# Depthwise convolution over 31 taps: three convolutions of half length over even tokens, odd tokens and their sum

## The chip, the cores and the metric

The kernel runs on one core of a Trainium2 chip. The metric is the device time of one execution in microseconds, the median of several runs. A core has five engines that work side by side, each through its own queue in order: TensorE (PE in the profile, PEld for its weight loads), VectorE (DVE), ScalarE (ACT), GpSimd (POOL) and SyncE (SP, which here only issues DMAs). TensorE writes into PSUM, from where VectorE or ScalarE must fetch the result before the bank is used again.

## The reference

One layer of a block with two branches that share an input projection; 1024 tokens, 1024 channels, 256 context tokens, all in float32. Cut to what matters here:

```
h  = rms_norm(x, g_pre) * (1 + sc) + sh
ua, gate_a, q, k, v, gate_b, gm = split(h @ w_in)
a, g = split(ua)                          # 1024 channels each
y = a * sigmoid(g)
y = conv(y, conv_w, padding 15) + conv_b  # each channel on its own, 31 taps along the tokens
y = silu(layer_norm(y, ln_g, ln_b)) * silu(gate_a)
y_conv = y @ w_conv_out
y_attn = (attention(q, k, v, ctx) * silu(gate_b)) @ w_attn_out
out = (sigmoid(ga) * y_conv + sigmoid(gb) * y_attn) @ w_out
x   = x + gt * rms_norm(out, g_post)
```

For one channel, output token t is the sum over i of w[i] * y[t + i - 15], where tokens outside 0 to 1023 count as zero.

## The kernel before

The kernel keeps channels on the 128 partitions and tokens along the free dimension, so a channel tile is 128 x 1024 and there are eight of them (KD = 8). Matrix products run on float32 values that are split in a high and a low part, three matmuls for each product (`mm3`, L119); the high part (`whi`) is a cast on ScalarE, the low part (`wlo`) a subtraction, on GpSimd in the first half of the program and on VectorE later (`wl`, L142 and L1397).

The program is written as one stream. `stream` (L172) loads, splits and multiplies one weight tile after the other; each tile is a job of two halves of 512 tokens, each half eight steps of three matmuls into a PSUM tile `ppj` with two buffers. `filler(n)` (L1304) does n such steps. Its jobs are the gates, and for each channel tile j of the convolution a `gate` (tanh on ScalarE to `ts`) and a `value` (`conv_jobs`, L741), which VectorE combines to `y`, the gated input of the convolution.

When `y` of a tile is complete, `conv_taps(j, y)` (L768) puts 31 entries on a list. The first is an activation on ScalarE that multiplies `y` with the middle tap and adds the bias. The other 30 are one `scalar_tensor_tensor` each on VectorE: accumulator = `y` shifted * tap weight + accumulator, over 1009 to 1023 tokens. The accumulator lies in PSUM (`pconv`) for the tiles that are done in the first half, and in SBUF (`acc`) from the moment `in_psum[0]` is set to False (L1384). With the last entry GpSimd adds the tile to `ysum` (for the mean of the layer norm) and it is written to DRAM (`accD`).

`pump(n)` (L737) takes n entries from the list and issues them. Where and how many is written by hand:

- In `work(n)` (L1310), after each step of filler, a share `RATE` of an entry: 0.25 while the context is normalised, 0.45 during `ctx_kv`, 0.2 while the weights of the first group are loaded, 0.5 behind the groups.
- In the loop over 4 groups and 4 quarters (L1348, sixteen blocks): a query/key/value product of 48 matmuls in two halves, then the rope of the block before (`qkv_rope` on VectorE), three entries, then `per` = 20 steps of filler with an entry behind those with i % 5 in (1, 3) and one more where q is odd. At i == 2 the block before is transposed (`qkv_tr`), at i == 4 VectorE and GpSimd make the reciprocal root (`stat`), at i == 9 ScalarE scales (`qkv_scale`, `qk`).
- Behind the loop: entries until none is in PSUM, `work(2)`, the rope of the last block, `work(12)`, its transposes; then one entry per two steps of filler (L1403), five more between the first row maxima, and the rest in `conv_rest` (L1436).

Up to L1394 every engine is held to the order of the program (`Ordered`, L41); behind it the framework may move instructions, with priority for those under `urgent()`. On the convolution follow the layer norm over `accD`, the attention loop, the output projections and the last product.

`gq`, the 64 gains of the query and the key norm, is loaded once at the start (L438, L439). `ctx_kv` uses the key gains (L565), and `rope_tables` (L452) folds both into the tables of the rope. Just behind the first step of `rope_tables` SP issues the weights of group 0 (`wgr`, L584 and L585).

Of the kernel before, what the change touches and what calls it, by code (L numbers as in the profile page):

```python
# [18 lines left out]
P = 128  # L19
D = 1024  # L20
T = 1024
CT = 256
KD = 8
NT = 8
HD = 64
NH = 16
NG = 4
TAPS = 31
PAD = 15
EPS = 1e-6  # L30
SCALE = HD ** -0.5
NKC = (T + CT) // P
# [3 lines left out]
def block_kernel(ctx: ExitStack, tc: tile.TileContext, x, cx, cc, wmod, bmodT, bmodg, vecs, gpost,  # L36
                 wkv, wq, wch, wco, wao, wout, convw, qg, kg, rcos, rsin, out):
    nc = tc.nc
    SP = nc.sync
# [27 lines left out]
    def tl(tag, shape, bufs, dtype=F32, pool="sb"):  # L67
        return pools[pool].tile(list(shape), dtype, tag=tag, bufs=bufs, name=nm(tag))
# [65 lines left out]
    cvb, lng, lnb, gpre = (vec[:, i, :] for i in range(4))  # L134
    bmT = const.tile([P, 16], F32, name="bmT")
    cw = const.tile([P, KD, TAPS], F32, name="cw")
    lngh = const.tile([P, KD], F32, name="lngh")
    lnbh = const.tile([P, KD], F32, name="lnbh")
    gq = const.tile([P, 2, HD], F32, name="gq")


    wl = [G]  # L142
# [295 lines left out]
    SP.dma_start(out=gq[:, 0, :], in_=qg.partition_broadcast(P))  # L438
    SP.dma_start(out=gq[:, 1, :], in_=kg.partition_broadcast(P))  # L439
# [12 lines left out]
    def rope_tables():  # L452
        tcos, tsin = tl("blk", (P, NT, 32), 4, pool="A"), tl("blk", (P, NT, 32), 4, pool="A")
        SP.dma_start(out=tcos[:], in_=rcos)
        SP.dma_start(out=tsin[:], in_=rsin)
        yield 6
        for i in range(2):
            CC = tl("rope", (P, NT, HD), 4, pool="A")
            SS = tl("rope", (P, NT, HD), 4, pool="A")
            for hh in range(2):  # L460
                a, b = hh * 32, (1 - hh) * 32
                V.tensor_tensor(out=CC[:, :, a:a + 32], in0=tcos[:, :, 0:32],
                                in1=gq[:, i, a:a + 32].unsqueeze(1).to_broadcast([P, NT, 32]), op=ALU.mult)
                V.scalar_tensor_tensor(out=SS[:, :, a:a + 32], in0=tsin[:, :, 0:32], scalar=(1.0 if hh else -1.0),
                                       in1=gq[:, i, b:b + 32].unsqueeze(1).to_broadcast([P, NT, 32]),
                                       op0=ALU.mult, op1=ALU.mult)
                yield 2
            rope.append((CC, SS))
# [64 lines left out]
    def ctx_kv():  # L533
# [31 lines left out]
        V.tensor_tensor(out=kv, in0=kv, in1=gq[:, 1, :].unsqueeze(1).to_broadcast([P, 2 * NG, HD]), op=ALU.mult)  # L565
        yield 8
        for gp in range(2):
            p = pt("m", (P, 256))
# [163 lines left out]

    ysum = tl("ysum", (P, T), 1)
    taps = []
    tap_ins = [None]

    def pump(n):  # L737
        for _ in range(min(n, len(taps))):
            taps.pop(0)()

    def conv_jobs(j):  # L741
        st = {}

# [24 lines left out]
    def conv_taps(j, y):  # L768
        st = {}

        def first():
            if not in_psum[0]:
                st["acc"] = tl("acc", (P, T), 2)
            else:
                if j == 0:
                    unshare(1)
                    share({"conv": 1})
                st["acc"] = pt("conv", (P, T))
                in_psum[1] = j + 1
            S.activation(st["acc"][:], y[:], AF.Identity, scale=cw[:, j, PAD:PAD + 1], bias=cvb[:, j:j + 1])  # L780

        def tap(i):
            o = i - PAD
            a, b = max(0, -o), min(T, T - o)
            acc = st["acc"]
            to = acc
            if in_psum[1] == j + 1 and (i == TAPS - 1 or not in_psum[0]):
                st["acc"] = to = tl("acc", (P, T), 2)
                for c, d in ((0, a), (b, T)):
                    if c < d:  # L790
                        S.copy(to[:, c:d], acc[:, c:d])
                in_psum[1] = 0
            tap_ins[0] = V.scalar_tensor_tensor(out=to[:, a:b], in0=y[:, a + o:b + o], scalar=cw[:, j, i:i + 1],
                                                in1=acc[:, a:b], op0=ALU.mult, op1=ALU.add)

        def last():
            acc = st["acc"]
# [7 lines left out]
        for i in range(TAPS):
            if i != PAD:
                taps.append(lambda i=i: tap(i))
        q = taps.pop()
        taps.append(lambda: (q(), last()))

    def tanh_job(src, dst):
        def ev(p, tok):
# [535 lines left out]
    for g in range(NG):  # L1348
        for q in range(4):
            mm = qkv_mm(g, q)  # L1350
            next(mm)
            if prev:
                qkv_rope(*prev)
            else:
                pump(3)
            next(mm)
            next(mm)
            pump(3)
            next(mm)
            due = 0 if q == 3 else 1 if (g, q) == (0, 0) else -1  # L1360
            if q == 2 and g < NG - 1:
# [225 lines left out]
```

## Time and profile before

| | before |
|---|---|
| median of 3 runs | 1412.09 us (1410.0 to 1413.3) |
| the profiled execution | 1411.38 us |
| its span, first to last instruction | 1409.6 us |
| mean granted TensorE clock | 0.989 |
| busy: PE, DVE, ACT, POOL | 1351.9, 1043.1, 564.7, 687.6 us |
| taps with the accumulator in PSUM | 197, 251.9 us of DVE |
| taps into or within SBUF (`acc`) | 43 |
| first and last tap | at 78.9 and 626.4 us |

Times of a row are in microseconds unless they are means of one instruction, which are in nanoseconds. A row of a group names the engine, the operation, the tile written and those read, the shape, the count, then busy time and mean, then the idle time of the engine just ahead of these instructions and what ended it. All engine operations have line L51, that of the helper that records them, so the tiles tell which is which: `pconv` and `acc` are the accumulators of the convolution, `y<-ts,ppj` the gate product, `ts<-ts,ppj` a silu, `ppj` a projection, `po` in the first half the query/key/value product, `ps<-kk,rq` and `mx` the row maxima, `ps<-r,kk` and `pe` the scores. PE counts as busy until the modelled end of a matmul, which overlaps with the next.

### The profile page before, as it was taken

Reading aid. Unit: us, or ns where it says so; the run is one execution under the profiler, and the core shown is the slowest. Engines: PE = TensorE matmul, PEld = TensorE weight load, DVE = VectorE, ACT = ScalarE, POOL = GpSimd, SP = SyncE. Lnnn points to the kernel's source line nnn. Section 1 sums busy time; section 2 is a strip of 40 time slices with the busy share of each in tenths; the row PEclk is TensorE's granted clock in tenths of the full one; section 3 lists DMA queues with packets and bytes.
Section 4 is the critical chain, followed back from the end, with each engine's and each line's share of the span. In section 5 each row is a group of like instructions: output and inputs, shape, how many; then the busy total and the mean of one; then the engine's idle time right before and its main releaser. Section 6 shows DMA issues by size and latency. Waiting matters only on the chain.

```text
span 1409.6 us, 19371 instructions
## 1 busy us (share of the span) xinstructions
PE 1351.9 (96%) x6520; PEld 1000.3 (71%) x6520; DVE 1043.1 (74%) x1359; ACT 564.7 (40%) x1388; POOL 687.6 (49%) x559
## 2 busy tenths in 40 slices
PE   5999999999999999999999999999999999999995
PEld 3768889887888877666666666666666565788774
DVE  3476988998889998885775566567676776349967
ACT  5542344343433332134444445445454434222333
POOL 1112257466556550054675556555556656263623
PEclk9999999999999999999999999999999999999998
DMA  9733434444444436523545444543365657699754
GB/s 317 272 127 105 137 109 159 140 167 150 136 144 134 152 111 185 163 90 116 177 152 171 135 120 147 183 144 120 113 197 173 214 194 263 218 315 347 242 186 154
DMA packets 153187, 242.41 MB, mean 172 GB/s; under 512 B 19792, under 2 KB 72572, under 8 KB 153088
## 3 DMA queue, kind: packets, MB, share of 16 engines
q1 hardware_dynamic: 139648, 218.03, 47.1%
q10 hardware_dynamic: 13440, 23.14, 5.6%
q8 instruction: 52, 0.85, 0.3%
q14 instruction: 47, 0.39, 0.1%
HBM read 161.46 MB, written 79.52 MB: 171 GB/s over the span
## 4 chain that ended last, share of the span: by engine, by line
PE 60%; DVE 16%; issue 7%; POOL 6%; DMA 5%; ACT 4%; SPq 1%; ACTq 1%; POOLq 0%; DVEq 0%
PE ppj L51 26%; PE ps L51 17%; PE po L51 14%; DVE pconv L51 7%; PE pm L51 3%; DVE t L51 2%; POOL wlo L51 2%; DVE qk L51 2%; DMA wm<-in_wmod 1%; DVE qkt L51 1%; POOL opw L51 1%; DVE acc L51 1%; ACT pe L51 1%; DVE r1st L51 1%; POOL y L51 1%
## 5 line engine op out<-in xcount | busy, mean ns | idle before, releaser
L51 PE MATMUL ppj<-t,whi 128*128 128x512 f32 x1728 | 621.0, 403 | 17.2 <-DVE y L51 9.1
L51 PEld LDWEIGHTS ppj<-t,whi 128*128 128x128 f32 x1728 | 327.8, 190 | 124.1 <-issue 36.5
L51 PE MATMUL ppj<-t,wlo 128*128 128x512 f32 x864 | 340.7, 394 | 0.0
L51 DVE TENSOR_REDUCE mx<-ps 128x1 f32<-128x512 f32 (+1 forms) x320 | 199.7, 682 | 109.8 <-PE ps L51 109.2
L51 ACT ACTIVATE pe<-ps 128x512 f32<-128x512 f32 x320 | 188.0, 597 | 191.8 <-PE ps L51 186.8
L51 DVE SCALAR_TENSOR_TENSOR pconv<-y,cw,pconv 128x1016 f32<-128x1016 f32 (+14 forms) x197 | 251.9, 1279 | 6.7 <-ACT pconv L51 2.0
L51 PE MATMUL ps<-r,kk 128*128 128x512 f32 (+1 forms) x640 | 199.9, 393 | 0.7 <-DMA r<-mr 0.7
L51 POOL TENSOR_TENSOR psum<-psum,pe 128x512 f32<-128x512 f32 x128 | 171.0, 1354 | 33.0 <-ACT pe L51 29.7
L51 PEld LDWEIGHTS ppj<-t,wlo 128*128 128x128 f32 x864 | 164.8, 191 | 29.3 <-issue 0.2
L51 PE MATMUL po<-pe,vt 128*64 128x512 f32 x640 | 144.4, 597 | 0.0
L51 PEld LDWEIGHTS ps<-r,kk 128*128 128x128 f32 (+1 forms) x640 | 120.3, 188 | 29.5 <-issue 0.8
L51 POOL TENSOR_TENSOR psum<-psum,part 128x512 f32<-128x512 f32 x64 | 90.6, 1417 | 100.7 <-DVE part L51 100.7
L51 POOL TENSOR_TENSOR wlo<-wraw,whi 128x512 fp32r<-128x512 f32 x59 | 79.8, 1361 | 118.7 <-ACT whi L51 117.1
L51 PE MATMUL po<-wgh,t 128*128 128x384 f32 x512 | 130.1, 335 | 0.0
L51 POOL TENSOR_TENSOR psum<-pe,pe 128x512 f32<-128x512 f32 x32 | 42.9, 1359 | 122.5 <-ACT pe L51 122.5
L51 PEld LDWEIGHTS po<-pe,vt 128*64 128x64 f32 x640 | 43.1, 136 | 81.0 <-issue 78.9
L51 PEld LDWEIGHTS po<-wgh,t 128*128 128x128 f32 x512 | 92.7, 188 | 1.4 <-ACT qk L51 0.2
L51 PE MATMUL po<-wgl,t 128*128 128x384 f32 x256 | 85.8, 335 | 0.3 <-DVE wgl L51 0.3
L51 ACT CAST whi<-wraw 128x512 fp32r<-128x512 f32 x112 | 68.7, 634 | 42.0 <-PE ppj L51 22.4
L51 DVE TENSOR_TENSOR part<-pe,pe 128x512 f32<-128x512 f32 x64 | 66.2, 1038 | 19.4 <-ACT pe L51 19.3
L51 DVE TENSOR_TENSOR wlo<-wraw,whi 128x512 fp32r<-128x512 f32 x53 | 45.7, 865 | 45.5 <-ACT whi L51 45.4
L51 PE MATMUL ps<-kk,rq 64*128 64x512 f32 (+1 forms) x384 | 67.9, 405 | 4.9 <-ACT pe L51 3.1
(211 smaller groups left out, 1776.9 us busy)
## 6 DMA issues: line engine op xcount, KB each, us to landing
wraw<-in_wch SPq DMA_DIRECT2D x96, 256.0 KB
opD<-opw SPq DMA_DIRECT2D x56, 256.0 KB
wm<-in_wmod SPq DMA_DIRECT2D x24, 512.0 KB
W<-opD SPq DMA_DIRECT2D x48, 256.0 KB
r1D<-r1st SPq DMA_DIRECT2D x32, 256.0 KB
y<-accD SPq DMA_DIRECT2D x16, 512.0 KB
r<-r1D ACTq DMA_DIRECT2D x32, 256.0 KB
opD<-acc SPq DMA_DIRECT2D x13, 512.0 KB
```

Source lines behind the costliest of these rows:

```text
L51: i = f(*a, **k)
```

## The change

The convolution is done on pairs of tokens. With E the even tokens, O the odd ones and w the taps, the even outputs are a convolution of E with the odd-numbered taps (15 of them) plus one of O with the even-numbered taps (16), and the odd outputs come from a convolution of E + O with the sums of neighbouring taps, from which the two others are subtracted. So there are three convolutions over 512 tokens, with about 15 taps each, and some instructions that put them together.

`gated` writes `y` so that E and O are two halves of a tile. A channel tile has 48 entries on the list:

- `first`: two activations on ScalarE, one for each accumulator half.
- 14 taps on E into half 0.
- `even_end` (GpSimd adds O to E in place) with the first tap on O; 13 more taps on O into half 1.
- `odd_end`: a product for the edge, the last tap on O, written over O, and a copy of one column on ScalarE.
- `evens`: a reduction over 8 elements, the even outputs (512 elements, every second one of the output) and one edge element.
- `turn`: half 0 becomes the sum of both results with the bias taken off.
- 15 taps on E + O with the weights `cs` into half 0.
- `last`: the odd outputs, then as before `ysum` and the store.

`place` moves the accumulator from PSUM to SBUF with a copy on ScalarE once `in_psum[0]` is False. `cs` holds the negated sums of neighbouring taps and is made at the start with `ncvb`. The tile `gq` is no longer constant: it takes a buffer of the rope tables and is loaded in `rope_tables`; the key gains are also loaded at the start in a tile `gk` for `ctx_kv`. The numbers of entries per step are changed: RATE 0.45, 0.75, 0.4 and 0.8 in place of 0.25, 0.45, 0.2 and 0.5; five and twelve entries in a block in place of three and eight or nine; two per two steps of filler in place of one.

```diff
+    V.scalar_tensor_tensor(out=cs[:, :, 0:15], in0=cw[:, :, 0:30:2], scalar=-1.0, in1=cw[:, :, 1:30:2], op0=ALU.mult,
+                           op1=ALU.subtract)
+    V.tensor_scalar_mul(cs[:, :, 15:16], cw[:, :, 30:31], -1.0)
+    V.tensor_tensor(out=cs[:, :, 16:17], in0=cw[:, :, 14:15], in1=cw[:, :, 15:16], op=ALU.add)
+    V.tensor_scalar_mul(ncvb[:], cvb, -1.0)
...
-    SP.dma_start(out=gq[:, 0, :], in_=qg.partition_broadcast(P))
-    SP.dma_start(out=gq[:, 1, :], in_=kg.partition_broadcast(P))
+    gk = tl("gk", (P, HD), 1, pool="st")
+    SP.dma_start(out=gk[:], in_=kg.partition_broadcast(P))
...
         SP.dma_start(out=tsin[:], in_=rsin)
+        gq = tl("blk", (P, NT, 32), 4, pool="A")[:, 0:4, :].rearrange("p (i a) b -> p i (a b)", i=2)
+        SP.dma_start(out=gq[:, 0, :], in_=qg.partition_broadcast(P))
+        SP.dma_start(out=gq[:, 1, :], in_=kg.partition_broadcast(P))
...
+    def gated(y, hf, t, p):
+
+        pairs = lambda ap: ap.rearrange("p (u r) -> p u r", r=2)
+        V.scalar_tensor_tensor(out=y[:, :, hf * 256:hf * 256 + 256].rearrange("p r u -> p u r"), in0=pairs(t[:]),
+                               scalar=1.0, in1=pairs(p[:]), op0=ALU.add, op1=ALU.mult)
...
     def conv_taps(j, y):
         st = {}
+        E, O = y[:, 0, :], y[:, 1, :]
+
+        def place():
+
+            if in_psum[1] == j + 1 and not in_psum[0]:
+                acc, n = st["acc"], 1 if "M" in st else 2
+                st["acc"] = tl("acc", (P, 2, 512), 2)
+                S.copy(st["acc"][:, 0:n, :], acc[:, 0:n, :])
+                in_psum[1] = 0
+            return st["acc"]
...
-            S.activation(st["acc"][:], y[:], AF.Identity, scale=cw[:, j, PAD:PAD + 1], bias=cvb[:, j:j + 1])
...
+            S.activation(st["acc"][:, 1, :], O, AF.Identity, scale=cw[:, j, 14:15])
+            S.activation(st["acc"][:, 0, :], E, AF.Identity, scale=cw[:, j, 15:16])
+
+        def even_end():
+
+            G.tensor_tensor(out=E, in0=E, in1=O, op=ALU.add)
+            st["edge"] = tl("edge", (P, 10), 2)
+
+        def tap(c, src, k, w):
+            o = k - 7
+            a, b = max(0, -o), min(512, 512 - o)
+            acc = place()[:, c, a:b]
+            V.scalar_tensor_tensor(out=acc, in0=src[:, a + o:b + o], scalar=w, in1=acc, op0=ALU.mult, op1=ALU.add)
+
+        def odd_end():
+
+            acc = place()
+            V.tensor_tensor(out=st["edge"][:, 0:8], in0=O[:, 0:8], in1=cw[:, j, 16:31:2], op=ALU.mult)
+            V.scalar_tensor_tensor(out=O[:, 0:511], in0=O[:, 1:512], scalar=cw[:, j, 16:17], in1=acc[:, 1, 0:511],
+                                   op0=ALU.mult, op1=ALU.add)
+            S.copy(O[:, 511:512], acc[:, 1, 511:512])
+            st["M"] = True
+
+        def evens():
+            acc = place()
+            st["out"] = tl("acc", (P, T), 2)
+            out = st["out"][:].rearrange("p (u r) -> p r u", r=2)
+            edge = st["edge"]
+            V.tensor_reduce(out=edge[:, 8:9], in_=edge[:, 0:8], axis=AX.X, op=ALU.add)
+            V.scalar_tensor_tensor(out=out[:, 0, 1:512], in0=acc[:, 0, 1:512], scalar=cvb[:, j:j + 1],
+                                   in1=O[:, 0:511], op0=ALU.add, op1=ALU.add)
+            V.scalar_tensor_tensor(out=out[:, 0, 0:1], in0=acc[:, 0, 0:1], scalar=cvb[:, j:j + 1], in1=edge[:, 8:9],
+                                   op0=ALU.add, op1=ALU.add)
+
+        def turn():
+            acc = place()
+            V.scalar_tensor_tensor(out=acc[:, 0, :], in0=acc[:, 0, :], scalar=ncvb[:, j:j + 1], in1=O,
+                                   op0=ALU.add, op1=ALU.add)
+
+        def last():
+            acc = place()
+            out = st["out"]
+            V.scalar_tensor_tensor(out=out[:].rearrange("p (u r) -> p r u", r=2)[:, 1, :], in0=E,
+                                   scalar=cs[:, j, 16:17], in1=acc[:, 0, :], op0=ALU.mult, op1=ALU.subtract)
...
+        ks = [k for k in range(16) if k != 7]
         taps.append(first)
+        taps.extend(lambda k=k: tap(0, E, k, cw[:, j, 2 * k + 1:2 * k + 2]) for k in ks[:-1])
+        taps.append(lambda: (even_end(), tap(1, O, 0, cw[:, j, 0:1])))
+        taps.extend(lambda k=k: tap(1, O, k, cw[:, j, 2 * k:2 * k + 1]) for k in ks[1:] if k != 8)
+        taps.append(odd_end)
+        taps.append(evens)
+        taps.append(turn)
+        taps.extend(lambda k=k: tap(0, E, k, cs[:, j, k:k + 1]) for k in ks)
+        taps.append(last)
...
             if prev:
                 qkv_rope(*prev)
             else:
-                pump(3)
+                pump(5)
             next(mm)
             next(mm)
-            pump(3)
+            pump(5)
...
                 filler(1)
-                if i % 5 in (1, 3) or (i == 10 and q % 2):
+                if i % 5 in (0, 1, 3):
                     pump(1)
...
     while NF - done[0] > NB + 16:
         filler(2)
-        pump(1)
+        pump(2)
```

More of the change, by code (lines that the diff above doesn't have):

```diff
@@ L28 @@
 TAPS = 31
-PAD = 15
 EPS = 1e-6
@@ L136, in block_kernel @@
     cw = const.tile([P, KD, TAPS], F32, name="cw")
+    cs = const.tile([P, KD, 17], F32, name="cs")
+    ncvb = const.tile([P, KD], F32, name="ncvb")
     lngh = const.tile([P, KD], F32, name="lngh")
     lnbh = const.tile([P, KD], F32, name="lnbh")
-    gq = const.tile([P, 2, HD], F32, name="gq")
     wl = [G]
@@ L564, in ctx_kv @@
         V.tensor_tensor(out=kv, in0=kv, in1=r[:].unsqueeze(2).to_broadcast([P, 2 * NG, HD]), op=ALU.mult)
-        V.tensor_tensor(out=kv, in0=kv, in1=gq[:, 1, :].unsqueeze(1).to_broadcast([P, 2 * NG, HD]), op=ALU.mult)
+        V.tensor_tensor(out=kv, in0=kv, in1=gk[:].unsqueeze(1).to_broadcast([P, 2 * NG, HD]), op=ALU.mult)
         yield 8
@@ L734, in block_kernel @@
     taps = []
-    tap_ins = [None]
     def pump(n):
@@ L745, in gate @@
             if hf == 0:
-                st["y"] = tl("y4", (P, T), 3)
+                st["y"] = tl("y4", (P, 2, 512), 3)
             st[hf] = tl("ts", (P, 512), 4)
@@ L750, in value @@
         def value(w, hf):
-            yield from proj(w, hT, hf, lambda p, tok: V.scalar_tensor_tensor(
-                out=st["y"][:, tok], in0=st[hf][:], scalar=1.0, in1=p[:], op0=ALU.add, op1=ALU.mult))
+            yield from proj(w, hT, hf, lambda p, tok: gated(st["y"], hf, st[hf], p))
             if hf:
@@ L757, in conv_first @@
     def conv_first():
-        y = tl("y4", (P, T), 3)
+        y = tl("y4", (P, 2, 512), 3)
         for hf in range(2):
-            tok = slice(hf * 512, hf * 512 + 512)
             t = tl("ts", (P, 512), 4)
             S.activation(t[:], p0[0, hf][:], AF.Tanh, scale=0.5)
-            V.scalar_tensor_tensor(out=y[:, tok], in0=t[:], scalar=1.0, in1=p0[1, hf][:], op0=ALU.add, op1=ALU.mult)
+            gated(y, hf, t, p0[1, hf])
         conv_taps(0, y)
@@ L769, in conv_taps @@
         st = {}
+        E, O = y[:, 0, :], y[:, 1, :]
[6 more added lines that the diff above has]
+            return st["acc"]
         def first():
             if not in_psum[0]:
-                st["acc"] = tl("acc", (P, T), 2)
+                st["acc"] = tl("acc", (P, 2, 512), 2)
             else:
@@ L777, in first @@
                     share({"conv": 1})
-                st["acc"] = pt("conv", (P, T))
+                st["acc"] = pt("conv", (P, 2, 512))
                 in_psum[1] = j + 1
-            S.activation(st["acc"][:], y[:], AF.Identity, scale=cw[:, j, PAD:PAD + 1], bias=cvb[:, j:j + 1])
[L782 to L791, printed above, removed]
+            S.activation(st["acc"][:, 1, :], O, AF.Identity, scale=cw[:, j, 14:15])
@@ new lines, in turn @@
+        def turn():
[7 more added lines that the diff above has]
+                                   scalar=cs[:, j, 16:17], in1=acc[:, 0, :], op0=ALU.mult, op1=ALU.subtract)
+            if in_psum[1] == j + 1:
@@ L792, in tap @@
                 in_psum[1] = 0
[L793 to L797, printed above, removed]
             if j == 0:
-                G.tensor_copy(ysum[:], acc[:])
+                G.tensor_copy(ysum[:], out[:])
             else:
-                G.tensor_tensor(out=ysum[:], in0=ysum[:], in1=acc[:], op=ALU.add)
-            SP.dma_start(out=accD[j][:], in_=acc[:])
+                G.tensor_tensor(out=ysum[:], in0=ysum[:], in1=out[:], op=ALU.add)
@@ L804, in conv_taps @@
+            SP.dma_start(out=accD[j][:], in_=out[:])
+        ks = [k for k in range(16) if k != 7]
         taps.append(first)
[L805 to L809, printed above, removed]
+        taps.extend(lambda k=k: tap(0, E, k, cw[:, j, 2 * k + 1:2 * k + 2]) for k in ks[:-1])
+        taps.append(lambda: (even_end(), tap(1, O, 0, cw[:, j, 0:1])))
+        taps.extend(lambda k=k: tap(1, O, k, cw[:, j, 2 * k:2 * k + 1]) for k in ks[1:] if k != 8)
@@ L1317, in work @@
                 owed[0] -= 1
-    RATE = 0.25
+    RATE = 0.45
     ck = ctx_kv()
@@ L1327, in block_kernel @@
         work(d)
-    RATE = 0.45
+    RATE = 0.75
     n = 0
@@ L1334, in block_kernel @@
             gate.pop(0)[1]()
-    RATE = 0.2
+    RATE = 0.4
     closed(stp)
@@ L1386, in block_kernel @@
         pump(1)
-    RATE = 0.5
+    RATE = 0.8
     work(2)
@@ L1437, in conv_rest @@
         while taps:
-            pump(1)
+            pump(2)
             yield 2
```

## The prediction

> **What bounds the kernel now.** I read the page first, then the busy times by stage, then what TensorE (PE) waits for in the stage in which the convolution runs, then the chain, and at last the timeline around the two longest PE waits.
>
> ```profile
> PE 1351.9 (96%) x6520; PEld 1000.3 (71%) x6520; DVE 1043.1 (74%) x1359; ACT 564.7 (40%) x1388; POOL 687.6 (49%) x559
> ...
> PE ppj L51 26%; PE ps L51 17%; PE po L51 14%; DVE pconv L51 7%; PE pm L51 3%; DVE t L51 2%; POOL wlo L51 2%; DVE qk L51 2%; DMA wm<-in_wmod 1%; DVE qkt L51 1%; POOL opw L51 1%; DVE acc L51 1%; ACT pe L51 1%; DVE r1st L51 1%; POOL y L51 1%
> ...
> 149.00:526.00 377.00, 369.83 (x1834) 324.50 (x1834) 344.92 (x387) 150.94 (x652) 211.27 (x219) 1.00 0.43 138
> 526.00:540.00 14.00, 9.24 (x32) 6.95 (x30) 11.70 (x16) 4.34 (x7) 1.26 (x1) 0.76 0.24 81
> 540.00:577.00 37.00, 34.81 (x144) 28.05 (x144) 31.01 (x31) 6.43 (x12) 2.39 (x1) 0.95 0.94 262
> 577.00:606.00 29.00, 27.32 (x109) 17.88 (x110) 27.09 (x41) 5.40 (x10) 0.00 (x0) 0.94 0.33 97
> 606.00:1240.00 634.00, 627.31 (x3010) 401.54 (x3011) 409.17 (x575) 281.19 (x490) 365.41 (x257) 1.00 0.51 165
> ```
>
> Columns of the stages: length, then busy PE, PEld, DVE, ACT, POOL, granted clock, DMA share, GB/s. From 149 to 526 us (the sixteen query/key/value blocks, with projections and taps between) VectorE (DVE) is busy 345 of 377 us, 91%, and yet PE is idle for only 7.2. Whether a busy PE is full there is seen in the chain:
>
> ```profile
> 459.55 11.58 PE ppj L51 x51
> 471.13 8.36 PE po L51 x48
> ...
> 514.57 1.30 DVE pconv L51
> 515.89 1.30 DVE pconv L51
> 517.22 1.30 DVE pconv L51
> ```
>
> 51 projection matmuls in 11.58 us are 0.227 us each, 48 of qkv 0.174 each, back to back. So PE sets the time; the 7% of the chain that goes through `pconv` is a second path that is almost as long, not time to be had. The most that a lighter DVE can give back is what PE loses to it:
>
> ```profile
> PE ppj L51 <- DVE y L51: 3.1, 3, 1.3
> PE ppj L51 <- DVE ts L51: 1.6, 2, 1.1
> PE pm L51 <- DVE qk L51: 1.4, 4, 0.5
> ```
>
> (PE's waits from 149 to 526: us, times, longest.) That is 6.1 us in the blocks. The one long wait comes right behind them, at the handover to attention:
>
> ```profile
> 525.87 0.39 PE L51 MATMUL ppj<-t,whi 128*128 128x512 f32 x1
> 527.07 0.59 ACT L51 ACTIVATE ts<-ppj 128x512 f32<-128x512 f32 x1
> 527.38 1.67 DVE L51 TENSOR_TENSOR qk<-qk,rope 128x512 f32<-128x512 f32 x1
> 529.08 0.82 DVE L51 TENSOR_TENSOR qk<-qk,qkt 128x640 f32<-128x640 f32 x1
> 529.83 0.68 DVE L51 SCALAR_TENSOR_TENSOR y<-ts,ppj 128x512 f32<-128x512 f32 x1
> 530.56 0.80 PE L51 MATMUL ppj<-t,whi 128*128 128x512 f32 x1 [4.30 <-DVE y L51]
> ```
>
> PE stands until 530.56 because the gate product `y`, which frees its PSUM bank, is queued on DVE behind the rope of the last block, and that behind taps. In 526 to 540 the granted clock is 0.76 as well: 0.24 of 14 us is 3.4 us more.
>
> **The taps: what they cost.**
>
> ```profile
> L51 DVE SCALAR_TENSOR_TENSOR pconv<-y,cw,pconv 128x1016 f32<-128x1016 f32 x14 | 17.9, 1280 | 0.4
> L51 DVE SCALAR_TENSOR_TENSOR t<-t,q,acc 128x512 f32<-128x512 f32 x4 | 2.8, 747 | 0.9 <-POOL q L51 0.9
> L51 DVE SCALAR_TENSOR_TENSOR ts<-ts,ppj 128x512 f32<-128x512 f32 x46 | 31.4, 683 | 22.8 <-ACT ts L51 15.0 <-PE ppj L51 7.7
> L51 DVE TENSOR_REDUCE mc<-mx 128x8 f32<-128x24 f32 x16 | 2.6, 166 | 0.0
> ```
>
> A tap of 1016 takes 1.280 us, and taps that add to one accumulator follow each other every 1.32 (514.57, 515.89, 517.22), so 0.04 above the duration. Before: 30 x 1.32 = 39.6 us a channel tile. After, counting every full-length instruction: 14 taps of the even part, 14 of the odd part, `odd_end`, `evens`, `turn`, 15 taps of the sum, `last` = 47, with 508 elements on average. Two rows of half length differ: 0.683 with a constant as scalar, 0.747 with one scalar per partition. All 47 have the latter. The step from 512 to 1016 then is 0.533 us for 504 elements, 1.06 ns each, so 508 elements take 0.743, and the pace is 0.785. 47 x 0.785 = 36.9, and three tiny ones (8 elements and fewer) at 0.166 + 0.04 = 0.6: 37.5 us. A channel saves 2.1 us, eight 17 us of DVE, 5%, though a quarter of the arithmetic goes. Bounds: at 0.683 it is 47 x 0.723 + 0.6 = 34.6, 40 us in all; the lower end is in the third rival.
>
> [...]
>
> **Where the 17 us fall.** The pump rates, counted through the loops: 23 of 31 entries of a channel are issued ahead of the blocks before, 41 of 48 after; in a block 3 + 8 or 9 = 11.5 against 5 + 12 = 17; behind the blocks 38 against 66. In DVE time: ahead 29.4 against 32.0, a block 14.7 against 13.3, behind 48.5 against 51.6. So the blocks get 1.4 us each, 22 in all (DVE 91% to 86%), and the stages on either side get 3 us more each.
> - Blocks: no wait there is longer than 1.3 us, and 1.4 us of relief in each block would end them all, but the burst right ahead of the transposes' evacuations is not shorter (5 + 2 taps of 0.785 = 5.5 against 4 of 1.32 = 5.3). I take 3.5 of the 6.1 us, bounds 0 and 6.1.
> - Handover: between the transposes and the rope of the last block stand 8 taps before (10.6 us) and 10 after (7.9). The entry that meets `in_psum` false is then `evens`: an ACT copy of one half, which waits for DVE and on which DVE waits, and one tap with its tiny ones, about as much as the tap of before with its copy. `y` comes 2.7 us earlier; nothing else holds it that long, ACT's `ts` is done at 527.66. The wait falls to 2 us, and I take half of the clock's 3.4: 2.7 + 1.7 = 4.4, bounds 0 and 4.8 + 3.4 = 8.2.
> - Behind: 3 us more on DVE from 540 to 606, where it has 8 us free but is nearly full at the row maxima. PE loses 3.9 us there now; I add 1.0, bounds 0 and 3.0.
>
> **What is moved.** `gq` is loaded with the rope tables now, and `kg` a second time early, as `gk`.
>
> ```profile
> L438 SPq DMA_DIRECT2D gq<-in_qg x1: 436/436/436, 43.0 to 43.0; - x1
> L439 SPq DMA_DIRECT2D gq<-in_kg x1: 482/482/482, 43.4 to 43.4; - x1
> ...
> 133.53 0.42 SPq L455 DMA_DIRECT2D blk<-in_rsin  x1
> 134.00 0.42 SPq L584 DMA_DIRECT2D wgr<-in_wkv  x1
> ...
> 140.65 0.96 DVE L51 TENSOR_TENSOR wgl<-wgr,wgh 128x768 fp32r<-128x768 f32 x1 [6.21 <-DMA wgr<-in_wkv]
> ...
> 142.26 0.50 PE L51 MATMUL ppj<-t,whi 128*128 128x512 f32 x1 [1.64 <-DVE y L51]
> ```
>
> Here SP issues without a pause, and the two loads of `gq` go in between `rsin` and the weights of group 0. DVE waits 6.21 us for these with a `y` behind it, and PE 1.64 for that `y`. 0.436 + 0.482 = 0.9 us goes straight on the path. Bounds 0.9 and 2.6, the latter if the longer wait costs clock as the one at 526 did (half of its 3.4).
>
> The rest I cost at nothing: four small DVE operations more at the start (they go between 62 and 76 us, where DVE waits for ACT, as in the first row below); ACT's two activations of 512 for one of 1024; and the sum of even and odd on POOL, 8 x 1.35 us, unless its waits matter (below).
>
> ```profile
> 71.90 0.69 DVE L51 SCALAR_TENSOR_TENSOR ts<-ts,ps 128x512 f32<-128x512 f32 x1 [1.31 <-ACT ts L51]
> ...
> L51 ACT ACTIVATE pe<-ps 128x512 f32<-128x512 f32 x320 | 188.0, 597 | 191.8 <-PE ps L51 186.8
> L51 ACT ACTIVATE pconv<-y,vec,cw 128x1024 f32<-128x1024 f32 x7 | 8.5, 1218 | 6.8 <-DVE acc L51 6.8
> L51 POOL TENSOR_TENSOR psum<-psum,pe 128x512 f32<-128x512 f32 x128 | 171.0, 1354 | 33.0 <-ACT pe L51 29.7
> ```
>
> 2 x 0.597 is 1.19 against 1.218. From 606 on the order of PE does not change and PE is busy for 627 of 634 us, so what is gained before it stays.
>
> **Sum.** The profiled execution took 1411.4 us, its span 1409.6. 1411.4 - 3.5 - 4.4 + 1.0 + 0.9 = 1405.4; the median of the runs is 0.7 above this execution: **1406**.
>
> **Rivals.**
> 1. **The order, not the load** (0.21). PE's waits stay because bursts and the handover's rope decide, not DVE's mean load. For it: the burst of 5.5 us above, and DVE's queue never empties. Against it: `y` at 529.83 stands at the end of 16 us without a pause on DVE. Then 1411.4 + 0.9 + 0.7 - 1 = 1412, no change.
> 2. **POOL stands for the sum** (0.17; slower). `even_end` overwrites E, so POOL waits for the last tap that reads it, with everything behind it in its queue: the low parts of weights and the power for the norm that ACT's `qk` waits for, with the evacuations behind it on ACT.
>
> ```profile
> POOL stat L51 <- DVE stat L51: 48.3, 11, 11.6
> POOL ysum L51 <- DVE acc L51: 26.8, 5, 16.4
> ...
> ACT qk L51 <- POOL stat L51: 51.8, 15, 4.8
> ```
>
> Today POOL waits so once a channel at its end, 5.4 us on average, 16.4 at most. The mechanism decides from about 5.4 us on, one projection (24 x 0.227), for PE has a second bank for that long. Two waits of the longest kind seen for `stat`, 11.6, each pass on 6.2: 1405.6 + 12.4 = 1418. Against it: POOL is busy only 56% in the blocks, and a DVE with less to do is less late.
> 3. **Writes with a stride** (0.09). `gated` writes elements alternately to two places 2 KB apart, `evens` and `last` write every second element: four instructions a channel. No row of before writes so. Bounds: nothing, and one more element time for each, 512 x 1.06 ns = 0.54 us; four of them are 2.2 us, all that a channel saves. I take nothing in the sum. At the upper bound DVE is where it was and the time 1412.
>
> [...]
>
> 4. **All waits go** (0.08): 1411.4 - 6.1 - 8.2 + 0.9 + 0.7 = 1399.
>
> **How the numbers follow.** The forecast has 0.45 (1402 to 1409). A measurement of this kernel tells about 0.2% from no change, 2.8 us. Faster: 0.45 + 0.08 = 0.53. Within: 0.21 and most of the third, 0.28. Slower: 0.17 and the rest, 0.19. The range goes from 1397, a little under the fourth, to 1417, which takes in half of the second; the forecast's own is 1402 to 1409.
>
> **What would show it.** Taps of about 508 elements at 0.74 us and a pace of 0.78 (0.68 or 1.0 would be wrong); some 46 x 8 of them; DVE busy near 323 of 377 us in the blocks, PE's waits for `y` and `ts` there half of what they were; the wait for `y` at the handover near 2 us; `wgr` waited for 0.9 us longer; `gated` as long as `y` now. I am wrong if PE's idle time in the blocks does not fall, if POOL's waits for DVE pass 11 us and ACT's `qk` with them, or if stages behind 606 change.

## Result, and the profile after

| | before | after |
|---|---|---|
| median, runs side by side | 1412.69 us (1410.0 to 1416.24, 6 runs) | 1422.62 us (1419.27 to 1424.99, 6 runs) |
| the profiled execution, its span | 1411.38, 1409.6 us | 1421.45, 1419.2 us |
| mean granted TensorE clock | 0.989 | 0.986 |

The ratio is 1.0066, with a 95% interval from 1.0046 to 1.0087. The change makes the kernel slower by about 10 us, where 1406 was forecast and 1417 was the upper end of the range. All engine operations now have line L50.

First the busy times on the page of after, then the stages by the same cuts as before (length, busy PE, PEld, DVE, ACT, POOL, clock, DMA share, GB/s):

```profile
PE 1353.1 (95%) x6520; PEld 1002.6 (71%) x6520; DVE 1030.8 (73%) x1523; ACT 566.4 (40%) x1398; POOL 699.4 (49%) x567
```

```profile
149.00:526.00 377.00, 372.34 (x1847) 329.27 (x1846) 332.77 (x507) 153.51 (x661) 219.75 (x226) 1.00 0.42 139
526.00:540.00 14.00, 14.00 (x64) 11.61 (x63) 13.59 (x21) 4.26 (x8) 0.00 (x0) 1.00 0.57 180
540.00:577.00 37.00, 32.64 (x135) 25.06 (x134) 20.91 (x33) 7.71 (x13) 2.79 (x1) 0.95 0.83 241
...
606.00:1240.00 634.00, 614.00 (x2928) 388.02 (x2928) 408.95 (x579) 275.46 (x480) 361.09 (x253) 0.98 0.50 159
...
606.00:625.00 19.00, 19.00 (x81) 11.37 (x81) 17.58 (x23) 6.60 (x13) 11.33 (x8) 0.93 0.17 55
625.00:639.00 14.00, 0.44 (x2) 0.01 (x2) 11.21 (x15) 0.60 (x1) 3.21 (x2) 0.64 0.11 15
639.00:643.00 4.00, 4.00 (x6) 1.87 (x7) 0.00 (x0) 0.78 (x2) 0.00 (x0) 0.54 0.54 213
```

Until 540 us the stages look as they should: DVE has 12 us less to do in the blocks (332.8 against 344.9, where 323 was forecast), and from 526 to 540 PE is busy throughout at clock 1.00, where it was busy 9.2 of 14 us at 0.76. Then two things are new. From 540 to 577 DVE does only 20.9 us of work, where it did 31.0: it has run dry. And from 625 to 639 PE stands still.

PE's list of waits (us in all, times, longest) names that one:

```profile
PE ps L50 <- POOL ysum L50: 13.6, 1, 13.6
PE ppj L50 <- DVE y L50: 7.7, 3, 3.5
PE ppj L50 <- DVE ts L50: 4.3, 2, 4.1
```

The matmul `ps<-ysum,ones` of the layer norm's mean waits for POOL's last sum over the channel tiles, and all of PE's queue stands behind it. Before, that matmul did not appear in this list.

How the two kernels stand against each other can be followed with matmuls that both have. PE does its 6520 matmuls in the same order in all of these kernels but e2, which moves those of the layer norm. For six matmuls the start in before was subtracted from the start in each other kernel, in one execution of each; the table shows what was gained (negative) or lost between one and the next. The six start at 124, 169, 526, 595, 651 and 1013 us in before. What stands at 124 varies by up to 4 us from run to run, also where nothing ahead of it was changed (e3), and the gain up to 526 by 1 us among the runs with the same blocks (after, e1, e2, e5, e6, e9).

| us against before | at 124 | to 169 | to 526 (blocks) | to 595 (handover, first maxima) | to 651 | to 1013 | whole span |
|---|---|---|---|---|---|---|---|
| after | -3.2 | +2.9 | -4.2 | -6.8 | **+19.7** | +1.1 | +9.6 |
| e1_first_early | -0.3 | +0.9 | -4.4 | -2.0 | +3.9 | +1.1 | -2.0 |
| e2_mean_later | +0.1 | +3.7 | -5.2 | -6.5 | +9.4 | +3.8 | +5.7 |
| e3_before_first_behind | -3.1 | 0.0 | +1.0 | -3.7 | **+19.9** | 0.0 | +17.6 |
| e4_gated_reads | +0.4 | +0.9 | -6.6 | -8.9 | +19.8 | +1.2 | +5.3 |
| e5_gq_behind | -2.4 | +3.7 | -5.0 | -6.1 | +19.8 | +1.1 | +13.0 |
| e6_own_buffer | -3.7 | +2.2 | -5.1 | -2.1 | +2.3 | +1.1 | -3.4 |
| e7_own_buffer_reads | -0.1 | +3.8 | -6.6 | -4.0 | +2.3 | +1.1 | -5.2 |
| e8_all | -1.9 | +0.7 | -5.5 | -3.8 | +2.4 | +1.1 | -7.4 |
| e9_no_pool_sums | -2.9 | +2.3 | -5.2 | -6.2 | +12.7 | +1.1 | +0.2 |

So up to 595 us after is 11 us ahead, and between 595 and 651 it loses 19.7. The stages above account for that: 13.6 us of wait, 0.07 of 19 us and 0.46 of 4 us of clock (3.2), and a wait of 2.2 us for row maxima at 604 (in the timeline below), together 19.0.

Where the lateness begins is seen in the timeline. First three rows of before: the activation `first` of the eighth tile, POOL's last sum and the matmul that asks for it, which found the sum ready.

```profile
530.54 1.24 ACT L51 ACTIVATE acc<-y,vec,cw 128x1024 f32<-128x1024 f32 x1 [2.88 <-DVE y L51]
627.74 2.39 POOL L51 TENSOR_TENSOR ysum<-ysum,acc 128x1024 f32<-128x1024 f32 x1 [3.79 <-DVE acc L51]
632.59 1.88 PE L51 MATMUL ps<-ysum,ones 128*128 128x512 f32 x4
```

Then the timeline of after, on DVE, ACT, POOL and PE in turn (start, busy time, instruction, and the idle time before it with what ended it):

```profile
538.46 1.53 DVE L50 SCALAR_TENSOR_TENSOR acc<-y,cs,acc 128x504 f32<-128x504 f32 x2
...
551.51 0.69 DVE L50 SCALAR_TENSOR_TENSOR ts<-ts,ppj 128x512 f32<-128x512 f32 x1 [8.11 <-ACT ts L50]
554.09 2.72 DVE L50 SCALAR_TENSOR_TENSOR acc<-y,cw,acc 128x505 f32<-128x505 f32 x4 [1.89 <-ACT acc L50]
...
597.75 5.79 DVE L50 SCALAR_TENSOR_TENSOR acc<-y,cw,acc 128x508 f32<-128x508 f32 x4
...
618.13 9.86 DVE L50 SCALAR_TENSOR_TENSOR acc<-y,cs,acc 128x505 f32<-128x505 f32 x8
...
543.02 1.15 ACTq L50 DMA_DIRECT2D r<-r1D  x2
544.21 3.34 ACTq L50 DMA_DIRECT2D rq<-r1D  x2
550.38 0.45 ACTq L50 DMA_DIRECT2D r<-r1D  x1
550.88 0.60 ACT L50 ACTIVATE ts<-ppj 128x512 f32<-128x512 f32 x1 [8.58 <-DMA rq<-r1D]
550.90 2.38 ACTq L50 DMA_DIRECT2D r<-r1D  x3
553.33 1.34 ACT L50 ACTIVATE acc<-y,cw 128x512 f32<-128x512 f32 x2 [1.85 <-issue]
...
636.61 2.34 POOL L50 TENSOR_TENSOR ysum<-ysum,acc 128x1024 f32<-128x1024 f32 x1 [10.73 <-DVE acc L50]
...
604.19 0.74 PE L50 MATMUL ps<-r,kk 128*128 128x512 f32 x2 [2.17 <-DVE mx L50]
...
639.00 3.78 PE L50 MATMUL ps<-ysum,ones 128*128 128x512 f32 x4 [13.56 <-POOL ysum L50]
```

The pool `acc` has two buffers. A tile of before uses one of them. A tile that is finished in SBUF now uses both, one as the accumulator and one as `st["out"]`, the output that `evens` begins. So `first` of the eighth tile finds no buffer until the last tap of the seventh is done, at 540.0. By then ACT has begun to issue the twelve loads of the attention's operands from `r1D`, and stands behind them; `first`, at 530.54 before, comes at 553.33. DVE has no tap to do meanwhile (idle 8.11 and 1.89 us). The taps that are late run into the attention, where four take 5.79 us in place of 3. The last tap ends at 636.5 where it ended at 627.7, and PE, which had come 11 us earlier, waits.

The wait of 13.6 us has two parts. Before, the sum was ready at 630.1, 2.5 us ahead of its matmul at 632.6. Now it is ready at 639.0, 8.8 us later, and PE asks for it at 625.4, 7.2 us earlier. So even with the sum at the old time PE would have waited 4.7 us, by an estimate from these rows: part of what was gained ahead of this matmul could not have been kept.

### The profile page after: what moved, and what is told of

It is laid out like the page before. It is cut to its first block, busy times and chain, and to the rows that moved or that the text cites. A ratio compares the mean times of both kernels' runs of the same rounds, so it can differ in the third digit from the quotient of the medians.

```text
span 1419.2 us, 19555 instructions
## 1 busy us (share of the span) xinstructions
PE 1353.1 (95%) x6520; PEld 1002.6 (71%) x6520; DVE 1030.8 (73%) x1523; ACT 566.4 (40%) x1398; POOL 699.4 (49%) x567
## 4 chain that ended last, share of the span: by engine, by line
PE 69%; DVE 17%; DMA 4%; issue 4%; ACT 3%; POOL 3%; SPq 1%; ACTq 0%; POOLq 0%; DVEq 0%
PE ppj L50 31%; PE po L50 18%; PE ps L50 17%; DVE pconv L50 4%; PE pm L50 3%; DVE acc L50 3%; DVE mx L50 2%; DVE t L50 1%; DVE qk L50 1%; DVE qkt L50 1%; DMA wm<-in_wmod 1%; POOL y L50 1%; DVE y L50 1%; DVE ts L50 1%; DMA x<-in_x 1%
## 5 line engine op out<-in xcount | busy, mean ns | idle before, releaser
L50 PE MATMUL ppj<-t,whi 128*128 128x512 f32 x1728 | 618.9, 403 | 15.1 <-DVE y L50 7.7
L50 PEld LDWEIGHTS ppj<-t,whi 128*128 128x128 f32 x1728 | 327.8, 190 | 120.4 <-issue 33.5
L50 PE MATMUL ppj<-t,wlo 128*128 128x512 f32 x864 | 341.1, 395 | 0.0
L50 DVE TENSOR_REDUCE mx<-ps 128x1 f32<-128x512 f32 (+1 forms) x320 | 199.7, 682 | 108.1 <-PE ps L50 107.7
L50 ACT ACTIVATE pe<-ps 128x512 f32<-128x512 f32 x320 | 187.7, 596 | 193.3 <-PE ps L50 186.7
L50 PE MATMUL ps<-r,kk 128*128 128x512 f32 (+1 forms) x640 | 202.9, 398 | 3.9 <-DVE mx L50 2.2
L50 POOL TENSOR_TENSOR psum<-psum,pe 128x512 f32<-128x512 f32 x128 | 174.3, 1380 | 37.7 <-ACT pe L50 34.7
L50 PEld LDWEIGHTS ppj<-t,wlo 128*128 128x128 f32 x864 | 164.7, 191 | 30.0 <-issue 0.5
L50 DVE SCALAR_TENSOR_TENSOR pconv<-y,cw,pconv 128x507 f32<-128x507 f32 (+5 forms) x196 | 146.9, 750 | 10.1 <-ACT pconv L50 4.9
L50 PEld LDWEIGHTS ps<-r,kk 128*128 128x128 f32 (+1 forms) x640 | 120.7, 189 | 33.7 <-DVE mx L50 2.6
L50 PE MATMUL po<-pe,vt 128*64 128x512 f32 x640 | 144.4, 597 | 0.0
L50 POOL TENSOR_TENSOR psum<-psum,part 128x512 f32<-128x512 f32 x64 | 90.3, 1413 | 106.2 <-DVE part L50 106.2
L50 POOL TENSOR_TENSOR wlo<-wraw,whi 128x512 fp32r<-128x512 f32 x59 | 79.1, 1347 | 119.1 <-ACT whi L50 100.3
L50 PE MATMUL po<-wgh,t 128*128 128x384 f32 x512 | 132.0, 339 | 0.0
L50 PEld LDWEIGHTS po<-pe,vt 128*64 128x64 f32 x640 | 43.1, 136 | 81.0 <-issue 79.0
L50 POOL TENSOR_TENSOR psum<-pe,pe 128x512 f32<-128x512 f32 x32 | 42.2, 1338 | 114.3 <-ACT pe L50 114.1
L50 PEld LDWEIGHTS po<-wgh,t 128*128 128x128 f32 x512 | 93.2, 188 | 1.4
L50 PE MATMUL po<-wgl,t 128*128 128x384 f32 x256 | 86.3, 337 | 0.0
L50 DVE TENSOR_TENSOR part<-pe,pe 128x512 f32<-128x512 f32 x64 | 64.4, 1009 | 24.1 <-ACT pe L50 20.1
L50 ACT CAST whi<-wraw 128x512 fp32r<-128x512 f32 x112 | 68.5, 633 | 29.8 <-PE ppj L50 18.2
L50 DVE TENSOR_TENSOR wlo<-wraw,whi 128x512 fp32r<-128x512 f32 x53 | 46.6, 879 | 43.6 <-ACT whi L50 43.5
L50 ACT ACTIVATE ts<-ppj 128x512 f32<-128x512 f32 x78 | 47.3, 608 | 58.8 <-PE ppj L50 35.3
```

Of the source, the lines that this page charges most:

```text
L50: i = f(*a, **k)
```

## The experiments

Each ratio is against runs of before that were made beside the experiment; their medians lie between 1410.9 and 1411.3 us.

**e1_first_early: the seventh tile is done sooner.** Behind the blocks more entries per step are issued, so that the buffer comes free ahead of ACT's loads.

```diff
-    RATE = 0.8
+    RATE = 1.4
```

> Changed kernel, but RATE at the handover is 1.4 in place of 0.8, so that the rest of the seventh channel tile and the first activation of the eighth are issued ahead of ACT's twelve loads of r1D, as in the kernel before. Theory A (the late start: that activation stood behind the loads on ACT, DVE ran dry from 543 to 554 us, the taps ended at 636 and PE waited 13.6 us for ysum): the activation starts before 540, the last tap ends before 622, PE's wait for ysum is under 2 us, the time 1403 to 1409. Rival B (contention: the taps of the last tile read and write SBUF and are slowed by POOL's sums, whenever they start): the last tap ends after 630, the wait stays above 8 us, the time 1416 or more. Rival C (the load: 3 us more for DVE behind the blocks): the time within 2 us of 1422.

Measured: 1409.59 us, ratio 0.9987 (0.9972 to 1.0002) against before. From the timeline on ACT and the stages:

```profile
539.85 1.34 ACT L50 ACTIVATE acc<-y,cw 128x512 f32<-128x512 f32 x2 [4.54 <-DVE acc L50]
```

```profile
526.00:540.00 14.00, 12.32 (x49) 9.84 (x50) 11.84 (x18) 1.88 (x4) 0.17 (x1) 0.88 0.23 75
540.00:577.00 37.00, 35.70 (x156) 28.24 (x154) 33.60 (x49) 10.08 (x19) 3.92 (x2) 1.00 0.95 255
```

`first` still waits for the seventh tile (4.54 us, by DVE's `acc`), but it is 13.5 us earlier and ahead of the loads. DVE is busy 33.6 of 37 us, the wait for `ysum` is gone from PE's list, and of the 19.7 us lost 3.9 are left. The time is just above the 1403 to 1409 us expected, and the last tap ends at 623.4 us, not before 622. Only the order was touched here, so the arithmetic of the change isn't what makes it slow. But most of the handover's gain is gone too (2.0 us in place of 6.8): the taps that were held back had made room there.

**e3_before_first_behind: the same lateness put into before.** The kernel before, with its two-buffer pool untouched, issues the eighth tile's `first` only behind the last load from `r1D`. The seventh tile's last six taps are written there too, but they run no later than before (the last ends at 537.0 us, 542.7 in before). The excerpt leaves out the lines that remember that load.

```diff
-    RATE = 0.5
+    RATE = 0.0
...
+    pump(6)
+    with tc.issue_after(load_end[0].ins):
+        pump(1)
```

> Kernel before (31 taps of full length), with one thing of the changed kernel: the activation that starts the eighth channel tile is held behind ACT's twelve loads of r1D. Theory A: DVE runs dry for 8 to 12 us there, the last tap ends at 634 to 640 in place of 628, PE waits 6 to 11 us for ysum, the time is 1418 to 1424. Rivals B and C: the time within 2 us of 1412.7.

Measured: 1430.47 us, ratio 1.0121 (1.0094 to 1.0148). Timeline on ACT, stage and PE's waits:

```profile
557.66 1.24 ACT L51 ACTIVATE acc<-y,vec,cw 128x1024 f32<-128x1024 f32 x1
```

```profile
540.00:577.00 37.00, 35.25 (x157) 28.36 (x156) 18.30 (x21) 7.91 (x13) 0.00 (x0) 1.00 0.87 246
```

```profile
PE ps L51 <- POOL ysum L51: 16.6, 1, 16.6
```

The old convolution with a late `first` shows the whole picture: DVE dry from 540 to 577, the wait for `ysum`, and +19.9 us between 595 and 651. That this is as much as in after is chance: the wait for the sum is longer here (16.6 us in place of 13.6), and PE has no wait for row maxima in that stretch. It is slower than expected, since `first` came 4 us later than in after and taps of 1.26 us drain no faster; and it has no gain from the blocks to set against it.

**e9_no_pool_sums: is it POOL that makes the taps slow?** In after, the sums that POOL makes of the attention's probabilities are left out for the first of the sixteen windows and a constant 1.0 stands for them.

```diff
-            G.tensor_tensor(out=acc_p[w, e][:], in0=prob[n - 1, e][:], in1=x[:], op=ALU.add)
-        elif c not in (0, 3, 8):
+            G.memset(acc_p[w, e][:], 1.0) if w == 0 else G.tensor_tensor(out=acc_p[w, e][:], in0=prob[n - 1, e][:], in1=x[:], op=ALU.add)
+        elif c not in (0, 3, 8) and w > 0:
...
+        if c in (4, 9) and w == 0:
+            part.pop((w, e))
```

> Changed kernel, but GpSimd leaves out its sums of the probabilities for the first of the sixteen attention windows (a constant stands in their place, so the first window's result is not that of the reference); the order of everything else stays. It takes away what slows the taps in SBUF from 596 to 626 us and leaves the late start. Theory A (the late start alone): PE's wait for ysum stays at 13 to 14 us, 1421 to 1423. Rival B (contention alone): the wait falls under 2 us, 1408 to 1411. Both in part, by the rows of the changed kernel (the taps from 618 to 628 at 1.67 in place of 0.76 us, 4 of the 8, and 3 of those from 597.8 to 603.5): 7 taps x 0.9 = 6 us less, a wait of 7 to 8, 1414 to 1418.

Measured: 1412.27 us, ratio 1.0008 (0.999 to 1.0027). DVE's timeline and PE's waits:

```profile
551.56 2.71 DVE L50 SCALAR_TENSOR_TENSOR acc<-y,cw,acc 128x505 f32<-128x505 f32 x4 [2.42 <-ACT acc L50]
...
597.16 3.08 DVE L50 SCALAR_TENSOR_TENSOR acc<-y,cw,acc 128x508 f32<-128x508 f32 x4
...
612.90 6.24 DVE L50 SCALAR_TENSOR_TENSOR acc<-y,cs,acc 128x505 f32<-128x505 f32 x8
```

```profile
PE ps L50 <- POOL ysum L50: 9.3, 1, 9.3
```

The taps still begin late, and they go at 0.77 us where four of them took 5.79 in after, and 6.24 us in place of 9.86 for the eight that follow. The loss between 595 and 651 falls from 19.7 to 12.7 us. So POOL's part is about 7 us, and the late start alone has 12.7; the median is under the 1414 to 1418 us that were expected for both in part. In e6_own_buffer, below, taps that are in time meet POOL's sums as well (six would take 4.6 us at 0.77 each):

```profile
597.73 8.26 DVE L50 SCALAR_TENSOR_TENSOR y<-y,cs,y 128x511 f32<-128x511 f32 x6
```

There PE does not wait for `ysum`, for the last tap ends at 618.7 us and the matmul comes at 626.3. So taps beside POOL's sums (POOL is busy 6.48 us from 595 to 606 there) are slow whether they are late or in time, and PE waits for `ysum` only where they are late. Taps with the accumulator in PSUM take 0.75 us in the blocks, though POOL is busy 220 of 377 us there; what makes the difference was not shown.

**e2_mean_later: who waits for the end of it.** The mean of the layer norm is asked for eight steps later.

```diff
-        yield 14
+        yield 22
```

> Changed kernel, but the matmul of the mean is issued eight steps of the attention loop later (22 in place of 14); the taps stay as they are. Theory A and rival B (both lose the time in that one wait of PE): eight steps are about 9.3 us of PE work, the wait for ysum falls from 13.6 to about 4, the time to 1412 to 1415. Rival C: no change, 1422.

Measured: 1415.45 us, ratio 1.0018 (1.0001 to 1.0035). POOL's timeline and PE's waits:

```profile
644.01 2.40 POOL L50 TENSOR_TENSOR ysum<-ysum,acc 128x1024 f32<-128x1024 f32 x1 [5.24 <-DVE acc L50]
```

```profile
PE ps L50 <- DVE mx L50: 7.2, 4, 3.8
```

The sum starts 7.4 us later still than in after, and yet PE no longer waits for it, where a wait of about 4 us was expected. Half of the 19.7 us come back. A good part of the rest stays because DVE now does late taps where the row maxima are due (7.2 us of waits for `mx`, 2.7 in after), and another 2.7 us go between 651 and 1013. Asking later helps; beginning in time helps more.

**e6_own_buffer: the cause mended.** The eighth tile's accumulator is taken from another pool, and nothing else changes.

```diff
-                st["acc"] = tl("acc", (P, 2, 512), 2)
+                st["acc"] = tl("y4", (P, 2, 512), 3)
```

> Changed kernel with one tag changed: the accumulator of the eighth channel tile takes the free third buffer of y4 in place of one of the two of acc, which the seventh tile holds both (accumulator and output) until its last tap. The rates stay. Theory A, in its closer form (the activation stood behind ACT's loads because it had to wait for that buffer): the activation starts by 535, DVE has no dry stretch of over 4 us from 526 to 577, the last tap ends before 615, PE's wait for ysum is under 1 us, PE keeps the 11 us that it was ahead at 595 us, the time is 1399 to 1404. Rival B (the taps in SBUF are slowed by POOL whenever they start): the last tap after 625, 1412 or more. Rival D (whatever is won up to 595 is lost again in the row maxima, as in the run with more taps at the handover): 1407 to 1411.

Measured: 1406.47 us, ratio 0.9967 (0.9949 to 0.9985). Timeline on ACT and DVE, stages, and PE's waits:

```profile
521.82 1.34 ACT L50 ACTIVATE y<-y,cw 128x512 f32<-128x512 f32 x2 [5.32 <-DVE y L50]
...
618.00 0.75 DVE L50 SCALAR_TENSOR_TENSOR acc<-y,cs,y 128x512 f32<-128x512 f32 x1
```

```profile
526.00:540.00 14.00, 11.21 (x38) 8.66 (x37) 11.21 (x18) 2.26 (x5) 0.00 (x0) 0.76 0.39 137
540.00:577.00 37.00, 34.30 (x149) 26.91 (x147) 33.61 (x47) 7.35 (x14) 4.45 (x2) 1.00 0.88 254
```

```profile
PE ppj L50 <- DVE y L50: 7.0, 3, 2.8
PE ppj L50 <- DVE ts L50: 5.6, 3, 2.8
```

With that one buffer `first` comes 31 us earlier, the last tap 18 us, no wait for `ysum` is in PE's list, and the change is faster than before. By the medians it is 16 us faster than after. It is slower than the 1399 to 1404 us expected: PE is 8.6 us ahead at 595 and not 11, and 2.3 us more go up to 651, 2.2 of them to one wait for row maxima, as rival D has it in part. The change's forecast of 1406 is met with this one buffer, but not by the forecast's sum: from 526 to 540 PE is idle for 2.8 us, for with the eighth tile's taps back in DVE's queue a silu `ts` is late there, and the clock is 0.76 as it was before.

**e4_gated_reads: the alternating writes.** `gated` reads PSUM and SBUF with a step of two and writes without one.

```diff
-        V.scalar_tensor_tensor(out=y[:, :, hf * 256:hf * 256 + 256].rearrange("p r u -> p u r"), in0=pairs(t[:]),
-                               scalar=1.0, in1=pairs(p[:]), op0=ALU.add, op1=ALU.mult)
+        V.scalar_tensor_tensor(out=y[:, :, hf * 256:hf * 256 + 256], in0=pairs(t[:]).rearrange("p u r -> p r u"),
+                               scalar=1.0, in1=pairs(p[:]).rearrange("p u r -> p r u"), op0=ALU.add, op1=ALU.mult)
```

> Changed kernel, but the gate product reads its inputs with a step of two elements and writes E and O in one piece each, in place of reading in one piece and writing alternately to two places. If only the alternate writes are dear, the 16 products take 0.68 to 0.75 us in place of 1.09, 6 us less of DVE in all; if every step costs, 1.1 or more. For the time theory A expects 1420 to 1423, since the long wait for ysum stays.

Measured: 1420.33 us, ratio 1.0052 (1.0032 to 1.0072). Groups of instructions in this kernel, then in after:

```profile
L50 DVE SCALAR_TENSOR_TENSOR y<-ts,ppj 128x512 f32<-128x512 f32 x14 | 9.5, 681 | 0.7 <-PE ppj L50 0.6
```

```profile
L50 DVE SCALAR_TENSOR_TENSOR y<-ts,ppj 128x512 f32<-128x512 f32 x14 | 15.2, 1085 | 0.7 <-PE ppj L50 0.6
L50 DVE SCALAR_TENSOR_TENSOR pconv<-y,cw,pconv 128x507 f32<-128x507 f32 x28 | 21.0, 750 | 0.8
L50 DVE SCALAR_TENSOR_TENSOR acc<-pconv,vec,y 128x511 f32<-128x511 f32 x6 | 4.5, 750 | 0.7 <-ACT y L50 0.6
L50 DVE SCALAR_TENSOR_TENSOR acc<-y,cs,pconv 128x512 f32<-128x512 f32 x6 | 4.5, 749 | 0.2
```

Writing alternately to two places costs 1085 - 681 = 0.40 us an instruction; reading with a step of two costs nothing (681 ns, and 680 in before without it). `evens` and `last` (`acc<-pconv,vec,y` and `acc<-y,cs,pconv`) write every second element and take 750 and 749 ns, as a tap does. In the blocks the gain is 6.6 us in place of 4.2. The median is 2.3 us below that of after, with intervals that overlap: the stall behind stays whole (+19.8).

**e5_gq_behind: the place of `gq`.** The two loads of `gq` are issued behind the weights of group 0.

```diff
+        yield 3
...
-        yield 6
+        yield 3
```

> Changed kernel, but the two loads of gq are issued behind the weights of group 0 and not ahead of them. The step of the prediction (0.9 us straight on the path there): PE reaches the first block 0.9 us earlier, between 127 and 150 us it loses 1 to 3 us less. For the whole time theory A expects at most 1 us of it back, 1421 to 1423, since the long wait for ysum takes up what comes ahead of it only in part; without an effect the stage from 76 to 149 us looks as in the changed kernel.

Measured: 1422.21 us, ratio 1.0073 (1.0044 to 1.0101), no different from after. Waits from 113 to 165 us, here and in after:

```profile
DVE wgl L50 <- DMA wgr<-in_wkv: 5.4, 1, 5.4
...
PE ppj L50 <- DVE y L50: 3.2, 1, 3.2
```

```profile
PE ppj L50 <- DVE y L50: 3.5, 1, 3.5
```

In before PE's wait there is 1.6 us. With `gq` out of the way it is still 3.2.

**e7_own_buffer_reads and e8_all: put together.** e7 is e6 with the edit of e4, e8 is e7 with the edit of e5.

> As e6_own_buffer, and the gate product with the steps in its reads (0.68 us in place of 1.09). The 6 us less of DVE lie under PE's work: theory A expects 1 to 3 us less than e6_own_buffer, 1397 to 1402; rival D the same as e6_own_buffer.

> As e7_own_buffer_reads, and gq loaded behind the weights of group 0: 1 to 3 us less again if the path ahead of the blocks is kept, 1395 to 1400; the same as e7_own_buffer_reads if the blocks make up for it.

Measured: 1406.28 us, ratio 0.9956 (0.9938 to 0.9974), and 1404.82 us, ratio 0.9953 (0.9937 to 0.9968). PE's waits from 149 to 526 us in e8:

```profile
PE ppj L50 <- DVE y L50: 1.9, 3, 1.2
PE ppj L50 <- DVE ts L50: 1.6, 2, 1.0
```

Both beat before. They are 4 to 5 us slower than theory A expected, and e7 comes out as e6, as rival D had it. e8 is the fastest of all, by 6.3 us against before and 17.4 against e5, which is as slow as after and ran on the same chip. No wait in the blocks is longer than 1.2 us there. Between e6, e7 and e8 the intervals overlap, so what e4's and e5's edits add to e6 isn't shown.

## Why the prediction was wrong, step by step

**Right: what a tap costs.** 0.743 us was worked out for 508 elements, 0.750 was measured, against 0.68 and 1.0 that would have been wrong. By an estimate from the prediction's rows of 512 and 1016 elements (0.750 less 508 x 1.06 ns), 0.21 us of it don't shrink with the length, and so halving the 1016 elements of 1.280 us saves little.

**Right, in mechanism and nearly in size: the blocks.** 3.5 us was taken of at most 6.1; from 169 to 526 after gained 4.2, and e4 6.6. DVE was to be busy 323 us there and was 332.8: 12 gate products cost 0.40 us more each, 5 us, and the rope of the last block now falls ahead of 526. The waits explain the gain of after. Before there were 6.1 us of them from 149 to 526; in after there are these, and one of the two is now the `y` of the handover:

```profile
PE ppj L50 <- DVE y L50: 4.2, 2, 2.1
```

That is 4.0 us less for the blocks proper, beside a gain of 4.2.

**Half right: the handover.** The wait for the last `y` fell from 4.3 to 2.1 us, "near 2 us" as forecast. Up to 595 after gained 6.8 us against 3.4 (4.4 less 1.0), with all 3.4 us of the clock from 526 to 540 back where half was taken. But that much is luck: it is there only while the eighth tile's taps are held back, and e3, with the old taps held back, gains 3.7 too. Where the taps are in time (e1, e6, e7, e8) it is between 2.0 and 4.0. In e6 PE's wait for `y` is 2.1 us as well, but its waits for the silu `ts` up to 606 are 5.0 us, where they were 2.8 before, and the clock from 526 to 540 stays at 0.76; the prediction did not name that silu.

**Wrong: what is behind 540.** The steps that failed are "Behind: 3 us more on DVE from 540 to 606 [...] I add 1.0, bounds 0 and 3.0" and "From 606 on the order of PE does not change [...] so what is gained before it stays." The order did hold (the mean's first matmul is PE's 2960th in both kernels); that the gain stays does not follow from it, for an instruction that keeps its place still waits for its operand, and the sooner it comes the longer: this one came at 625.4 us and started at 639.0. The load on DVE was counted, and it was not the load: 19.7 us went. The step looked at how many entries are issued, and not at what the first of them needs. Three things in the text of the kernel were passed over: that `evens` takes a second buffer of a pool of two; that the one who asks next is an activation on ACT, with a queue of its own that takes twelve loads from 536 to 553; and that PE's next instruction for the convolution, the mean's matmul, stands in order among the attention's. e3 puts the late `first` alone into before and gets the 19.9 us, e6 takes the lack of a buffer alone away and gets 17.4 of the 19.7 back. The bound of 3.0 would have needed "and unless the taps begin later".

**The rivals.** The order, not the load (1412): not in the blocks, where PE was idle for 7.2 us and is for 4.7, the handover's 2.1 among them; what the order decided lay behind 540, which the rival did not name. POOL as the bound in the blocks (1418) didn't happen: its longest wait for `stat` there fell from 11.6 to 6.5 us. That 1422 lies near 1418 is chance; the slowdown came from another place. Of the strided writes, the alternating ones cost 0.40 us (1085 against 681 ns), near the upper bound of 0.54, the step of two nothing (750 and 749 ns, as a tap). In time the alternating writes are worth 1 to 2 us in the blocks: without them e4 and e7 gain 6.6 us there and e8 5.5, the six runs with them 4.2 to 5.2. All waits gone (1399) was not reached by the median of any version.

**The 0.9 us for `gq`.** PE's wait grew from 1.6 to 3.5 us, within the bounds of 0.9 and 2.6. But e5 says that `gq` is not why, and the longer wait for `wgr` did not come (DVE waits 5.8 us there, 6.2 before). Between 124 and 169 us the runs with the change lose from 0.7 to 3.8 us, e3 with the old convolution nothing. What it is stays open, as does a drift of 1.1 us between 651 and 1013 that every run with the change shows (e2 more).

## What to carry to other kernels

When a change gives an item one more buffer of a small pool, look for the next one to ask for a buffer, for the queue its first instruction stands in, and for what is queued ahead of it there. And where a result of work that runs beside is joined by an instruction in the order of the bounding engine, count when it is ready against when it is asked for; whatever was gained ahead of the join makes that instruction come earlier and the wait longer.

## What was unexpected of the hardware

A VectorE write that alternates between two places 2 KB apart took 1085 ns for 512 elements in after, against 681 ns without in e4. A step of two cost nothing in a read (681 ns, 680 without) or in a write (750 and 749 ns, as a tap). In after, SBUF taps of about 508 elements took 0.75 us, and up to 1.66 us while POOL made its sums; four in a row took 5.79 us there, and 3.08 in e9 without these sums. ACT issued loads of `r1D` between 543 and 553 us in after, with its arithmetic standing behind them for 8.58 us.
